# Stick-breaking attention by cumulated weights and differences of neighbouring values, in a decoder layer on one core

## The chip, the cores and the metric

The kernel runs on one core of a Trainium2 chip. The metric is the device time of one execution in microseconds (us). The kernel before was run three times: 3147.09 us in the median, 3140.37 lowest, 3151.94 highest.

Five engines work side by side, each through its own instruction stream in order: TensorE (PE in the profile, with PEld for its weight loads), VectorE (DVE), ScalarE (ACT), GpSimd (POOL) and SyncE (SP), which here issues nearly all DMAs.

## The reference, cut to what matters

One decoder layer on 2048 tokens of width 1024, in fp32: a normalised, modulated input is projected to queries, keys and values of 8 heads with forgetting attention ("fox") and 8 heads with stick-breaking attention ("sb"), each of width 64; both outputs are normalised per head and projected back, then follows a gated MLP with a short convolution, and a final norm. The change touches stick-breaking attention:

```python
z = einsum('bhqd,bhkd->bhqk', q_blk, k) * scale
strict = kpos[None, :] < qpos[:, None]
log_one_minus_beta = where(strict, log_sigmoid(-z), 0.0)
rest = cumsum(log_one_minus_beta, axis=3, reverse=True) - log_one_minus_beta
a = where(strict, exp(log_sigmoid(z) + rest), 0.0)
out = einsum('bhqk,bhkd->bhqd', a, v)
```

In words: with beta = sigmoid(z), key s gets the weight A(s) = beta(s) times the product of (1 - beta(j)) over all keys j between s and the query. Keys at or behind the query get none.

## The kernel before, in words

**Stages.** The attention stage comes first (0 to about 1600 us of the profile), then the output projection, the MLP's up-projection and its down-projection. The attention stage is a list of 32 units (L576), first 16 of sb, then 16 of fox: for each kind four head pairs p, and for each pair four blocks tb of 512 tokens. While a unit's attention (attend, L468) is recorded, the projection of the next unit (proj_gen, L580) is recorded between its steps by interleave (L131). A scheduler then orders the recorded instructions of each engine by a simulated timeline; each engine runs its list in that order. All matrix operands are split into a high part and a rest (split, L43: ACT writes the high part, then DVE or POOL subtracts).

**Projection of a unit** (finish_proj, L283). Queries and keys first (q, k), then, for even p, the values of two head pairs at once: matmuls at L320 into PSUM, then the split at L330 on ACT and DVE straight from PSUM into the tiles V (this pair) and V1, which L337 stores to DRAM for the next pair; for odd p, L307 loads it from there. For the first pair (sb, 0) the columns of the forget gate ride along, and each 128-token tile is done by itself (step 1); other even pairs do two tiles at a time. The input h comes through tiles named hp, 10 buffers; for (sb, 0) norm_proj (L353) computes them, and its split has its subtraction on POOL for tb > 0. Weights are split in load_w (L250), for sb with the subtraction on DVE (L252).

**Stick-breaking, one head and two query tiles of 128** (sb_head, L400). Keys go in chunks of up to 512 from the right (nearest to the query) to the left. For each chunk and query tile: two matmuls give -z in PSUM (L378, L379); ACT writes r = sigmoid(-z), which is 1 - beta, and a = sigmoid(z), which is beta (L410, L411). In the chunk on the diagonal (right is None) POOL sets one column to 0 (L415), and a DVE scan (L416) multiplies r up from the right, with a maximum against edge, whose identity part restarts it at the diagonal with 1. In a further chunk POOL copies the last product of the chunk to the right into the extra column (L418) and the scan (L419) goes on from it. Then a is multiplied by the product (L420): on DVE where (ch + qi) % 4 == 0, else on POOL. That is A.

**Weights times values** (weighted, L382), shared with fox: four 128x128 transposes on PE (L388) into PSUM, ACT copies the high part (L392), DVE subtracts (L393), and four matmuls (L397) with V add to the head's output. The head's end is L506 (ACT) and L507 (DVE), then head_var squares the output on POOL (L480).

**Queues.** SP issues the DMAs in its own order: q and k rearranged (L293, L303), hp (L346, L366), V (L307, L337), weights (L256). A DMA that has to wait holds those behind it on SP.

Of the kernel before, what the change touches and what calls it, by code (L numbers as in the profile page):

```python
# [8 lines left out]
F32 = mybir.dt.float32  # L9
# [3 lines left out]
ALU = mybir.AluOpType  # L13
# [3 lines left out]
P = 128  # L17
S = 2048
D = 1024
KT = D // P  # L20
HD = 64
NH = 8
NPAIR = 8
TB = 512
NTB = S // TB
# [8 lines left out]
def kernel(ctx: ExitStack, tc: tile.TileContext, x, c, w_ada, b_ada, g_attn, w_in, b_fgate,  # L34
                      g_out_fox, g_out_sb, w_out, g_mlp, w_up, conv_w, conv_b, w_down, g_final, out):
    nc = tc.nc
    x, out = x[0], out[0]
    w_ada, w_in, w_out, w_up, conv_w, w_down = w_ada[0], w_in[0], w_out[0], w_up[0], conv_w[0], w_down[0]

    def f(t):  # L40
        return t.bitcast(F32)

    def split(hi, lo, src, lo_engine=None):  # L43
        nc.scalar.activation(hi, src, AF.Copy)  # L44
        (lo_engine or nc.gpsimd).tensor_sub(lo, src, f(hi))  # L45

    const = ctx.enter_context(tc.tile_pool(name="const", bufs=1))
    dram = ctx.enter_context(tc.tile_pool(name="dram", bufs=1, space=DRAM))
# [7 lines left out]
    x1s = [dram.tile([P, D], F32, name=f"x1s{t}") for t in range(S // P)]  # L56
    vs = {k: [[dram.tile([P, 4, 2, P], F32, name=f"vs_{k}{p}_{t}") for t in range(NTB)] for p in range(2)]
          for k in ("sb", "fox")}
    zs = [dram.tile([4 * NH, P], F32, name=f"zs{t}") for t in range(NTB)]
    log_f = dram.tile([NTB * NH, TB], F32, name="log_f")  # L60
    fs = dram.tile([NH, S], F32, name="fs")
# [3 lines left out]
    edge = const.tile([P, TB + 1], F32, name="edge")  # L65
# [92 lines left out]
    sb = open_pool("sb", side="right")  # L158
    px = open_pool("px", side="right")
# [19 lines left out]
    def wide():  # L179
        return f(h_tile()).rearrange("p a n -> p (a n)")  # L180
# [68 lines left out]

    def load_w(kind, p):  # L250
        base = (0 if kind == "fox" else 3 * 512) + p * P
        lo_engine = nc.vector if kind == "sb" else None  # L252

        def load(tag, kt, first, step):
            raw = sl_.tile([P, 2, P], F32, name=f"raw_{tag}", tag="wraw", bufs=3)
            nc.sync.dma_start(raw, w_in[kt * P:(kt + 1) * P, first:first + (step + 1) * P].rearrange(  # L256
                "p (a n) -> p a n", n=P)[:, 0:step + 1:step, :])
            n = 2 * P + (NH if tag == "v" else 0)
            w_ = sl_.tile([P, 2, n], F32R, name=f"w_{tag}", bufs=8)
            w = w_[:, :, 0:2 * P].rearrange("p s (a n) -> p s a n", n=P)  # L260
            split(w[:, 0], w[:, 1], raw, lo_engine)
            if tag == "v" and (kind, p) == ("sb", 0):
                split(w_[:, 0, 2 * P:], w_[:, 1, 2 * P:], wfr[:, kt], nc.vector)
            return w if tag == "qk" else w_

        def load_qk(kt):
            qk_.append(load("qk", kt, base, 4))

        def load_v():
            return [load("v", kt, base + 1024, 1) for kt in range(KT)] if p % 2 == 0 else None  # L270

        qk_ = []
        if (kind, p) == ("sb", 0):
            return [qk_, load_qk, load_v]
        for kt in range(KT):
            load_qk(kt)
        return [qk_, load_v()]
# [5 lines left out]
    def finish_proj(kind, p, tb, aq, w, hts, res, ak=None):  # L283
        Q = sb.tile([P, 2, 2, TB], F32R, name="Q", bufs=2)
        K = sb.tile([P, 2, TB], F32R, name="K", bufs=5)
        V = sb.tile([P, 4, 2, P], F32R, name="V", bufs=6)
        q2 = sl_.tile([P, 2, TB], F32R, name="q2", bufs=2)
        k2 = sl_.tile([P, 2, TB], F32R, name="q2", bufs=2)
        nc.scalar.activation(q2[:, 0], aq, AF.Copy, scale=-HD ** -0.5)
        nc.vector.scalar_tensor_tensor(q2[:, 1], aq, -HD ** -0.5, f(q2[:, 0]), ALU.mult, ALU.subtract)  # L290
        for h in range(2):
            for r in range(2):
                nc.sync.dma_start(f(Q[r * HD:(r + 1) * HD, h]), f(q2[h * HD:(h + 1) * HD]))  # L293
        if ak is None:
            ak = pj()
            for kt in range(KT):
                accumulate(ak, 1, w[0], hts[kt], kt)
                if kt % 2:
                    yield
        split(k2[:, 0], k2[:, 1], ak, nc.vector)  # L300
        for h in range(2):
            for r in range(2):
                nc.sync.dma_start(f(K[r * HD:(r + 1) * HD, h]), f(k2[h * HD:(h + 1) * HD, r]))  # L303
        yield
        spill = vs[kind][p // 2][tb]
        if p % 2:
            nc.sync.dma_start(f(V), spill)  # L307
        else:
            V1 = sb.tile([P, 4, 2, P], F32R, name="V", bufs=6)
            forget = (kind, p) == ("sb", 0)  # L310
            step, width = (1, 2 * P + NH) if forget else (2, 2 * P)
            if forget:
                zn = px.tile([P, 4, NH], F32, name="zn", bufs=1)
            for i in range(0, 4, step):
                av = pj()
                for t in range(step):
                    tok = slice((i + t) * P, (i + t + 1) * P)
                    for kt in range(KT):
                        for m, (a, bb) in enumerate(((0, 0), (0, 1), (1, 0))):
                            nc.tensor.matmul(av[:, t * width:(t + 1) * width], hts[kt][:, a, tok],  # L320
                                             w[1][kt][:, bb, 0:width],
                                             start=kt == 0 and m == 0, stop=kt == KT - 1 and m == 2)
                        if kt % 4 == 3:
                            yield
                if forget:
                    nc.vector.tensor_copy(zn[:, i], av[:, 2 * P:width])
                av = av[:, 0:step * 2 * P].rearrange("p (t e h d) -> p t e h d", t=step, e=2, h=2)
                for e, v in enumerate((V, V1)):
                    v = v[:, i:i + step]
                    split(v[:, :, :, 0:HD], v[:, :, :, HD:P], av[:, :, e], nc.vector)  # L330
            if forget:
                b = pt()
                nc.tensor.transpose(b[0:4 * NH, 0:P], zn.rearrange("p t n -> p (t n)"), ident)
                zt = px.tile([4 * NH, P], F32, name="zt", bufs=1)
                nc.scalar.activation(zt, b[0:4 * NH, 0:P], AF.Identity, bias=bf_c)
                nc.sync.dma_start(zs[tb], zt)
            nc.sync.dma_start(spill, f(V1))  # L337
        res.append((Q, K, V))
        yield

    def proj(kind, p, tb, w, res):
        hts = []
# [57 lines left out]
    def sb_head(j, qc, hl, Q, K, V, o):  # L400
        n = (2 * j + 2 + 3) // 4
        right = [None, None]
        for ch in range(n - 1, -1, -1):
            at = []
            for qi in range(2):
                need = min(512, (2 * j + qi + 1) * P - ch * 512)
                b = logits(max(need, 2 * P), slice((qc + qi) * P, (qc + qi + 1) * P), hl, Q, K[ch])
                r = sx.tile([P, 512 + 1], F32, name="r", bufs=7)
                a = sx.tile([P, 512], F32, name="a", bufs=7)
                nc.scalar.activation(r[:, :need], b[:, :need], AF.Sigmoid)  # L410
                nc.scalar.activation(a[:, :need], b[:, :need], AF.Sigmoid, scale=-1.0)  # L411
                rev = r[:, 0:need + 1][:, ::-1]
                if right[qi] is None:

                    nc.gpsimd.memset(r[:, need:need + 1], 0.0)  # L415
                    nc.vector.tensor_tensor_scan(rev, rev, edge[:, TB - need:TB + 1][:, ::-1], 0.0, ALU.mult, ALU.max)  # L416
                else:
                    nc.gpsimd.tensor_copy(r[:, need:need + 1], right[qi][:, 0:1])  # L418
                    nc.vector.tensor_tensor_scan(rev, rev, rev, 1.0, ALU.mult, ALU.bypass)  # L419
                (nc.vector if (ch + qi) % 4 == 0 else nc.gpsimd).tensor_mul(a[:, :need], a[:, :need], r[:, 1:need + 1])  # L420
                right[qi] = r
                at.append(a)
            yield
            nk = min(4, 2 * j + 2 - 4 * ch)
            for m in range(0, nk, 2):
                kts = [4 * ch + m, 4 * ch + m + 1]
                weighted(o, kts, lambda kt, qi: at[qi][:, (kt - 4 * ch) * P:(kt - 4 * ch + 1) * P], V, hl,
                         ch == n - 1 and m == 0, ch == 0 and m == nk - 2, kts[0] == 2 * j)
                yield
# [225 lines left out]
    sx = open_pool("sx", side="right")  # L655
# [3 lines left out]
    for i, u in enumerate(units):  # L659
        kind, p, tb = u  # L660
# [3 lines left out]
        if u == ("fox", 0, 0):  # L664
            tick(1 << 20)
            close_pool("sx", "px")
            sx = open_pool("fx", side="right")
# [6 lines left out]
        if kind == "fox":  # L674
            n = sum(2 * (2 + 2 * tb + j2 + 1) for j2 in range(2)) + 1
        else:
            n = sum(2 * (tb + 1 + 2 * tb + j2 + 1) for j2 in range(2)) + 1
# [205 lines left out]
    for sblk in range(2):  # L883
# [21 lines left out]
        a, b = bank_a(), bank_a()  # L905
# [44 lines left out]
    for tb in range(NTB):  # L950
# [13 lines left out]
        for k in range(NKD):  # L964
            g, w = load(k, tb)
# [55 lines left out]
```

## Time and profile before

| | |
|---|---|
| time, median of 3 runs | 3147.09 us (3140.37 to 3151.94) |
| span of the profiled execution (no other time of it is listed) | 3139.3 us |
| PE busy | 2967.0 us, 95% |
| PE weight loads busy | 2511.6 us, 80% |
| DVE busy | 2145.5 us, 68% |
| ACT busy | 1691.0 us, 54% |
| POOL busy | 1227.1 us, 39% |
| mean granted TensorE clock | 0.983 |
| instructions | 46425 |

How to read it: busy time is the union of an engine's instructions. PE's matmuls overlap one another and their ends are modelled, so a busy PE isn't PE at its peak. Shares over the whole span mix stages: sb attention ends near 910 us, fox attention near 1600 us, and the rest is projections and MLP. A row of a group gives the line, the engine, the operation, output and inputs, the shape, the count, then busy us, mean ns of one, idle time of the engine ahead of it and what ended that. The line of a helper (split is L44 and L45) stands for all its callers; the tile names tell them apart.

### The profile page before, as it was taken

What the parts mean: (1) busy time and instruction counts of PE and PEld (TensorE: products, weight loads), DVE (VectorE), ACT (ScalarE), POOL (GpSimd) and SP (SyncE); (2) the same over time, 40 slices, a digit from 0 to 9 for tenths busy, and PEclk for the clock granted to TensorE, in tenths of its full rate; (3) what the DMA queues carried; (4) which work ended last, traced back from release to release, by engine and by line L of the source; (5) the groups of instructions that cost most, each with busy time, mean ns of one, the idle gap of its engine ahead of it and who ended that gap; (6) DMA issues with size and microseconds to landing.
All of it is one profiled execution on the core that took longest, in us unless ns stands there. A gap on an engine that the chain in (4) does not pass through costs nothing. (4 is left out here: it accounts for less than half of the span.)

```text
span 3139.3 us, 46425 instructions
## 1 busy us (share of the span) xinstructions
PE 2967.0 (95%) x15934; PEld 2511.6 (80%) x15934; DVE 2145.5 (68%) x3342; ACT 1691.0 (54%) x3161; POOL 1227.1 (39%) x1387
## 2 busy tenths in 40 slices
PE   6889998989989999999999999999899998999998
PEld 5778787877878889888877678888678887888887
DVE  6787888878875876556843587778987776354253
ACT  5666776666756676567744444444444444343332
POOL 1554455456553242242212344344444442322321
PEclk8999999999999999999999999999999999999999
DMA  9547542555336696585446632222222223554552
GB/s 267 177 140 255 168 136 69 182 185 155 123 108 221 214 314 211 158 313 162 164 158 222 212 97 86 86 83 83 82 82 89 85 81 130 190 199 161 189 199 90
DMA packets 292940, 496.51 MB, mean 158 GB/s; under 512 B 29448, under 2 KB 177664, under 8 KB 291680
## 3 DMA queue, kind: packets, MB, share of 16 engines
q1 hardware_dynamic: 281072, 480.92, 47.9%
q10 hardware_dynamic: 11632, 12.63, 1.1%
q8 instruction: 126, 2.06, 0.3%
q14 instruction: 110, 0.90, 0.1%
HBM read 352.61 MB, written 90.51 MB: 141 GB/s over the span
## 5 line engine op out<-in xcount | busy, mean ns | idle before, releaser
L810 PE MATMUL ps_o<-oa,wu 128*128 128x512 f32 x2088 | 503.5, 392 | 14.4 <-DVE oa L45 6.9
L810 PEld LDWEIGHTS ps_o<-oa,wu 128*128 128x128 f32 x2088 | 390.5, 188 | 105.5 <-DVE oa L45 10.7
L397 PE MATMUL ps_pv<-at,V 128*128 128x256 f32 x2304 | 410.9, 296 | 41.6 <-DVE at L393 24.8
L393 DVE TENSOR_TENSOR at<-ps_pt,at 128x512 fp32r<-128x512 f32 (+1 forms) x576 | 366.0, 653 | 102.8 <-ACT at L392 99.8
L281 PE MATMUL ps_pj<-hp,w_qk 128*128 128x512 f32 x1512 | 418.4, 406 | 11.1 <-ACT hp L44 3.1
L420 POOL TENSOR_TENSOR a<-a,r 128x512 f32<-128x512 f32 (+3 forms) x240 | 283.4, 1182 | 368.8 <-DVE r L416 112.3
L392 ACT ACTIVATE at<-ps_pt 128x512 fp32r<-128x512 f32 (+1 forms) x576 | 319.4, 577 | 179.8 <-PE ps_pt L388 147.3
L397 PEld LDWEIGHTS ps_pv<-at,V 128*128 128x128 f32 x2304 | 337.0, 192 | 84.6 <-DVE at L393 42.8
L281 PEld LDWEIGHTS ps_pj<-hp,w_qk 128*128 128x128 f32 x1512 | 275.7, 191 | 65.4 <-POOL hp L45 4.0
L45 DVE TENSOR_TENSOR wd<-wdraw,wd 128x1024 fp32r<-128x1024 f32 x88 | 112.4, 1277 | 261.4 <-ACT wd L44 261.4
L378 PE MATMUL ps_qk<-K,Q 128*128 128x512 f32 (+2 forms) x640 | 264.1, 414 | 11.3 <-DMA K<-q 5.8
L419 DVE TENSOR_TENSOR_SCAN r<-r 128x513 f32<-128x513 f32 x192 | 258.0, 1355 | 21.7 <-ACT r L410 14.5
L45 POOL TENSOR_TENSOR g<-graw,g 128x512 fp32r<-128x512 f32 x84 | 141.3, 1684 | 326.8 <-ACT g L44 326.8
L960 PE MATMUL ps_o<-wd,g 128*128 128x512 f32 x1040 | 250.8, 391 | 8.8 <-ACT g L44 8.8
L810 PE MATMUL ps_t<-ob,wu 128*128 128x512 f32 x984 | 243.2, 392 | 0.0
L320 PE MATMUL ps_pj<-w_v,hp 128*128 128x256 f32 (+1 forms) x1536 | 234.1, 291 | 4.8 <-DVE q L45 2.2
L379 PE MATMUL ps_qk<-K,Q 128*128 128x512 f32 (+2 forms) x640 | 238.1, 373 | 0.0
L960 PEld LDWEIGHTS ps_o<-wd,g 128*128 128x128 f32 x1040 | 196.2, 189 | 50.0 <-ACT g L44 9.2
L44 ACT ACTIVATE wu<-wuraw 128x512 fp32r<-128x512 f32 x214 | 133.2, 626 | 185.5 <-PE ps_o L810 111.5
L320 PEld LDWEIGHTS ps_pj<-w_v,hp 128*128 128x128 f32 x1536 | 211.8, 193 | 15.5 <-DVE q L45 3.1
L810 PEld LDWEIGHTS ps_t<-ob,wu 128*128 128x128 f32 x984 | 186.2, 189 | 39.4 <-DVE wu L45 0.3
L388 PE MATMUL ps_pt<-edge,a 128*128 128x128 f32 x1088 | 187.3, 281 | 27.6 <-POOL a L420 14.7
(217 smaller groups left out, 5743.3 us busy)
## 6 DMA issues: line engine op xcount, KB each, us to landing
hp<-hs SPq DMA_DIRECT2D x224, 512.0 KB
wuraw<-in_w_up_dram SPq DMA_DIRECT2D x84, 512.0 KB
wdraw<-in_w_down_dram SPq DMA_DIRECT2D x84, 512.0 KB
Q<-q SPq DMA_DIRECT2D x128, 256.0 KB
g<-u SPq DMA_DIRECT2D x42, 512.0 KB
graw<-g SPq DMA_DIRECT2D x84, 256.0 KB
hs<-hp SPq DMA_DIRECT2D x32, 512.0 KB
K<-q SPq DMA_DIRECT2D x128, 128.0 KB
```

The source lines that it names most:

```text
L45: (lo_engine or nc.gpsimd).tensor_sub(lo, src, f(hi))
L281: nc.tensor.matmul(acc, w[kt][:, a, n], h[:, bb], start=kt == 0 and i == 0, stop=kt == KT - 1 and i == 2)
L320: nc.tensor.matmul(av[:, t * width:(t + 1) * width], hts[kt][:, a, tok], w[1][kt][:, bb, 0:width], start=kt == 0 and m == 0, stop=kt == KT ...
L378: nc.tensor.matmul(b[:, :cw], Q[:, hl, 0, qcols], K[:, hl, :cw], start=True, stop=False)
L379: nc.tensor.matmul(b[:, :cw], Q[:, hl, 1, qcols], K[:, hl, :cw], start=False, stop=True)
L392: nc.scalar.activation(at[:, 0, lo:], b[:, lo:], AF.Copy)
L393: nc.vector.tensor_sub(at[:, 1, lo:], b[:, lo:], f(at[:, 0, lo:]))
L397: nc.tensor.matmul(o[:, 0:2 * P], V[kt // 4][:, kt % 4, hl, :], rhs, start=first and kk == 0 and w == 0, stop=last and kk == 1 and w == 1)
L419: nc.vector.tensor_tensor_scan(rev, rev, rev, 1.0, ALU.mult, ALU.bypass)
L420: (nc.vector if (ch + qi) % 4 == 0 else nc.gpsimd).tensor_mul(a[:, :need], a[:, :need], r[:, 1:need + 1])
L810: nc.tensor.matmul(b, w[:, p, j], o[:, q], start=first and i == 0, stop=last and i == 2, skip_group_check=True)
L960: nc.tensor.matmul(banks[t][n], g[:, a, t * P:(t + 1) * P], w[:, b, n * TB:(n + 1) * TB], start=k == 0 and i == 0, stop=k == NKD - 1 and i ...
```

## The change

With the cumulated weight C(s) = A(s) + A(s+1) + ... up to the query, summation by parts gives sum A(s) v(s) = sum C(s) (v(s) - v(s-1)), with v(-1) = 0. C follows the recurrence C(s) = beta(s) + (1 - beta(s)) C(s+1), from C = 0 at the query. So the scan becomes one multiply-add from the right, with r as the factor and a as the summand, written into a; the chunk to the right gives its first element as the scan's start value, by a pointer. Memset, column copy and product (L415, L418, L420) go. In the diagonal chunk POOL sets a to 0 where the key isn't ahead of the query (affine_select on the last 128 columns).

V now holds differences, split as before. For each sb value projection (p = 0 and 2, four blocks each) DVE copies the values from PSUM into an SBUF tile vr; SP stores vr to a DRAM buffer vd one row further down, stores its last row as the first of the next block's buffer, and loads the 512 rows from row 0 back as the tile before; POOL subtracts; then ACT and POOL split the difference into V and V1. The split's subtraction for the values moves from DVE to POOL, and that of the sb weights for p = 1, 2, 3 too.

```diff
+    vd = [[dram.tile([TB + 1, 2 * P], F32, name=f"vd{g}_{t}") for t in range(NTB)] for g in range(2)]
...
-        lo_engine = nc.vector if kind == "sb" else None
+        lo_engine = nc.vector if (kind, p) == ("sb", 0) else None
...
+            if kind == "sb":
+                vr = value_tile(p)
...
-                for e, v in enumerate((V, V1)):
-                    v = v[:, i:i + step]
-                    split(v[:, :, :, 0:HD], v[:, :, :, HD:P], av[:, :, e], nc.vector)
+                if kind == "sb":
+                    nc.vector.tensor_copy(vr[:, i:i + step], av.rearrange("p t e h d -> p t (e h d)"))
+                else:
+                    for e, v in enumerate((V, V1)):
+                        v = v[:, i:i + step]
+                        split(v[:, :, :, 0:HD], v[:, :, :, HD:P], av[:, :, e], nc.vector)
+            if kind == "sb":
+                steps_of_values(p // 2, tb, vr, V, V1)
+                yield
...
+    def value_tile(p):
+        t = wide() if p == 0 else px.tile([P, D], F32, name="xt", tag="xt", bufs=4)
+        return t.rearrange("p (i n) -> p i n", n=2 * P)
+
+    def steps_of_values(g, tb, vr, V, V1):
+        own = vd[g][tb]
+        nc.sync.dma_start(own[1:TB + 1].rearrange("(i p) n -> p i n", p=P), vr)
+        if tb == 0:
+            nc.sync.dma_start(own[0:1], edge[0:1, 0:2 * P])
+        if tb + 1 < NTB:
+            nc.sync.dma_start(vd[g][tb + 1][0:1], vr[P - 1:P, 3])
+        before = value_tile(2 * g)
+        nc.sync.dma_start(before, own[0:TB].rearrange("(i p) n -> p i n", p=P))
+        nc.gpsimd.tensor_sub(vr, vr, before)
+        dv = vr.rearrange("p t (e h d) -> p t e h d", e=2, h=2)
+        for e, v in enumerate((V, V1)):
+            split(v[:, :, :, 0:HD], v[:, :, :, HD:P], dv[:, :, e])
...
-                r = sx.tile([P, 512 + 1], F32, name="r", bufs=7)
+                r = sx.tile([P, 512], F32, name="r", bufs=7)
...
-                rev = r[:, 0:need + 1][:, ::-1]
                 if right[qi] is None:
-
-                    nc.gpsimd.memset(r[:, need:need + 1], 0.0)
-                    nc.vector.tensor_tensor_scan(rev, rev, edge[:, TB - need:TB + 1][:, ::-1], 0.0, ALU.mult, ALU.max)
-                else:
-                    nc.gpsimd.tensor_copy(r[:, need:need + 1], right[qi][:, 0:1])
-                    nc.vector.tensor_tensor_scan(rev, rev, rev, 1.0, ALU.mult, ALU.bypass)
-                (nc.vector if (ch + qi) % 4 == 0 else nc.gpsimd).tensor_mul(a[:, :need], a[:, :need], r[:, 1:need + 1])
-                right[qi] = r
+                    nc.gpsimd.affine_select(out=a[:, need - P:need], in_=a[:, need - P:need], pattern=[[-1, P]],
+                                            base=-1, channel_multiplier=1, compare_op=ALU.is_ge, fill=0.0)
+                rev = a[:, 0:need][:, ::-1]
+                nc.vector.tensor_tensor_scan(rev, r[:, 0:need][:, ::-1], rev,
+                                             0.0 if right[qi] is None else right[qi][:, 0:1], ALU.mult, ALU.add)
+                right[qi] = a
```

## The prediction

> **What bounds the kernel now.** I read first the page's busy shares in 40 slices of 78.5 us, to see the stages; the change touches only slices 1 to 12, the sb stage.
>
> ```profile
> PE   6889998989989999999999999999899998999998
> DVE  6787888878875876556843587778987776354253
> POOL 1554455456553242242212344344444442322321
> PEclk8999999999999999999999999999999999999999
> ```
>
> PE is at 8 or 9 tenths almost everywhere, DVE at 8 in the sb slices: two engines near their limit together. The sum by stretches says how near.
>
> ```profile
> core 0: us, PE busy (x) PEld busy (x) DVE busy (x) ACT busy (x) POOL busy (x), PEclk, DMA share, GB/s
> 130.00:910.00 780.00, 706.27 (x4485) 615.08 (x4484) 659.98 (x889) 528.71 (x1156) 419.42 (x595) 0.98 0.48 152
> 910.00:1580.00 670.00, 654.39 (x4300) 584.57 (x4298) 442.64 (x1137) 439.07 (x835) 211.97 (x283) 0.99 0.66 215
> ```
>
> The first row is sb, the second fox, the same kind of work on PE (logits, transposes, weighted values, projections). In sb PE is busy 90.5% and DVE 84.6%; in fox 97.7% and 66.1%. The change leaves PE's instructions as they are, so in this stage it can win at most PE's idle 73.7 us (780 - 706.3) and, to fox's share, 780 - 706.27/0.977 = 57 us. What ended the idle time is in the waits of PE from 100 to 910 us:
>
> ```profile
> PE ps_pv L397 <- DVE at L393: 23.3, 32, 1.3
> PE ps_pt L388 <- POOL a L420: 14.7, 20, 1.9
> PE ps_pv L397 <- DVE oT L507: 7.2, 7, 1.9
> ...
> PE ps_pt L388 <- DVE a L420: 2.3, 5, 0.6
> ```
>
> The columns are us in total, times, longest. The removed product is named for 17.0 us. The 30.5 us on L393 and L507 are waits for short DVE operations that stood behind longer ones in DVE's queue: they go with DVE's load, not with one line.
>
> **What DVE loses and gains.** Groups of DVE from 0 to 910 us (count, busy us, mean ns), then the single durations of the second scan (min, median, max):
>
> ```profile
> L419 DVE TENSOR_TENSOR_SCAN r<-r 128x513 f32<-128x513 f32 x192 | 258.0, 1355 | 21.7 <-ACT r L410 14.5 <-POOL r L418 4.1 <-POOL r L415 1.2
> L393 DVE TENSOR_TENSOR at<-ps_pt,at 128x512 fp32r<-128x512 f32 x222 | 146.5, 678 | 33.5 <-ACT at L392 32.7
> L420 DVE TENSOR_TENSOR a<-a,r 128x512 f32<-128x512 f32 x56 | 47.1, 841 | 4.2
> L416 DVE TENSOR_TENSOR_SCAN r<-r,edge 128x513 f32<-128x513 f32 x32 | 43.6, 1363 | 6.8 <-ACT r L410 6.6
> ...
> L45 DVE TENSOR_TENSOR w_qk<-raw_qk,w_qk 128x256 fp32r<-128x256 f32 x32 | 20.8, 660 | 5.4 <-ACT w_qk L44 5.2
> ...
> L45 DVE TENSOR_TENSOR V<-ps_pj,V 128x256 fp32r<-128x256 f32 x24 | 9.6, 408 | 0.9 <-ACT V L44 0.9
> L45 DVE TENSOR_TENSOR V<-ps_pj,V 128x128 fp32r<-128x128 f32 x32 | 8.9, 282 | 5.5 <-ACT V L44 5.3
> L45 DVE TENSOR_TENSOR w_v<-raw_v,w_v 128x256 fp32r<-128x256 f32 x16 | 7.9, 508 | 1.3 <-ACT w_v L44 1.3
> L420 DVE TENSOR_TENSOR a<-a,r 128x384 f32<-128x384 f32 x8 | 6.4, 804 | 0.5
> ...
> L420 DVE TENSOR_TENSOR a<-a,r 128x256 f32<-128x256 f32 x8 | 3.4, 423 | 0.5
> ...
> L420 DVE TENSOR_TENSOR a<-a,r 128x128 f32<-128x128 f32 x8 | 2.4, 306 | 0.4
> ```
> ```profile
> L419 DVE TENSOR_TENSOR_SCAN r<-r x192: 1192/1226/2309, 120.8 to 906.7; 128x513 f32<-128x513 f32 x192
> ```
>
> - The 80 products on DVE go: 47.1 + 6.4 + 3.4 + 2.4 = 59.3 us.
> - The scans stay, 320 of them, one element shorter. Multiply-add isn't in this trace; multiply-max with a second tensor (L416) and multiply alone (L419) cost the same, 1363 and 1355 ns, so the second operation costs nothing and I take 1226, the median of L419: its excess, 192 x 0.129 + 32 x 0.137 = 29 us, lies beside POOL's work, most of which goes, and I count 20. The bounds of this term: no excess lost (0), all lost (29); and a dearer addition (below).
> - Weight splits to POOL: 24 x 0.660 + 8 x 0.508 = 19.9 us.
> - The splits of the sb values go: 32 x 0.282 + 16 x 0.408 = 15.6 us. The copies from PSUM come: 16 of 128x256 at 0.408, the row of that shape, and 8 of 128x512 at 0.678, by L393, which reads PSUM in that shape; 12.0 us.
>
> Net 59.3 + 20 + 19.9 + 15.6 - 12.0 = 103 us off DVE, of 660. ACT's two splits of 512 columns in place of six or four smaller ones change it by some us either way, counted as nothing beside its 68% load in this stretch.
>
> **What POOL loses and gains.** The groups of POOL, 0 to 910 us, and the durations of the column copy:
>
> ```profile
> L420 POOL TENSOR_TENSOR a<-a,r 128x512 f32<-128x512 f32 x168 | 220.9, 1315 | 256.2 <-DVE r L419 84.7 <-ACT a L411 58.0 <-DVE r L416 24.2
> L418 POOL COPY r<-r 128x1 f32<-128x1 f32 x192 | 94.0, 492 | 1.9 <-DVE r L416 1.2
> L45 POOL TENSOR_TENSOR hp<-hf_a,hp 128x512 fp32r<-128x512 f32 x24 | 37.8, 1581 | 4.4 <-ACT hp L44 4.4
> ...
> masks.py:199 POOL TENSOR_SCALAR_AFFINE_SELECT edge<-edge 128x128 f32<-128x128 f32 x1 | 0.3, 294 | 0.1
> ```
> ```profile
> L418 POOL COPY r<-r x192: 176/186/2230, 118.0 to 905.6; 128x1 f32<-128x1 f32 x192
> ```
>
> 315 us go with the first two rows alone. In come 128 selects of 128x128 at 0.294 (38 us), 32 weight splits (20 us on DVE, here perhaps 25) and, for each of 8 value blocks, a subtraction of 1024 columns (2 x 1.32) and two of 512 (1.32 to 1.58), 5.5 us each, 44 in all. POOL falls from 419 to about 210 of 780 us; it is no bound. But L418's one column takes 186 ns in the median and 2230 at worst: a POOL instruction waits out a scan. The selects can be held likewise; each stands ahead of its scan, where a memset without a producer stood. Between 0.294 and 2.23 I take L418's mean excess of 0.3, or 0.6 us a select, and no net charge, as the product behind the scan, 1.3 us in the longest form, goes from the same chain. [...]
>
> **The values' new way through DRAM.** Before, one ACT and one DVE operation stood between a value matmul and V, the latter 0.28 or 0.41 us by the rows above. Now a copy, a store, a load, a subtraction and the splits follow. The nearest rows are in the order of time on SP, ACT and DVE:
>
> ```profile
> 284.11 0.32 SPq L239 DMA_DIRECT2D log_f<-fe  x1
> 284.52 1.80 SPq L346 DMA_DIRECT2D hp<-hs  x4
> 287.39 0.63 SPq L244 DMA_DIRECT2D fl<-log_f  x2
> ```
> ```profile
> 296.28 1.19 DVE L245 TENSOR_TENSOR_SCAN fc<-fl 8x512 f32<-8x512 f32 x1
> ```
> ```profile
> 1603.71 0.81 SPq L733 DMA_DIRECT2D x<-x1s  x2
> ...
> 1606.95 1.06 ACT L93 ACTIVATE junk_m<-x 128x1024 bf16<-128x1024 f32 x1 [2.09 <-DMA x<-x1s]
> ```
>
> A store that a load waits for takes at most 287.39 - 284.11 = 3.3 us; a 512 KB load 1606.95 - 1603.71 = 3.2 us; behind four loads of hp, a small one no more than 296.28 - 287.39 = 8.9 us. So the chain is 0.4 + 3.3 + 3.2 + 2.6 + 1.2 + 1.5 = 12 us, 18 with such traffic. The built program's order on PE has moved to meet it: in the first unit the first matmul on V stands behind 26 projection matmuls of 512 columns that stood behind it before, and some 40 transposes where there were some 20. By the next fences one such matmul is 226 ns (442 in 100 us of a saturated stretch) and a transpose 187.3/1088 = 0.17 us, so 26 x 0.226 + 40 x 0.17 = 13 us of PE work lie between the last value matmul and the first use, in place of some 3; the other even units are alike.
>
> ```profile
> 2300.00:2400.00 100.00, 100.00 (x442) 82.40 (x441) 78.25 (x88) 43.61 (x62) 46.56 (x33) 1.00 0.26 80
> ```
> ```profile
> L388 PE MATMUL ps_pt<-edge,a 128*128 128x128 f32 x1088 | 187.3, 281 | 27.6 <-POOL a L420 14.7
> ```
>
> Per block the lateness is between 0 and 18 - 13 = 5 us; I take 1, as the trip without traffic fits: 8 x 1 = 8 us of PE stall, bounds 0 and 40. What waits behind it: the subtraction waits for the load on POOL, and in the built order selects of the next chunks and the splits of hp stand behind it; a DVE scan waits for each select and PE for hp. On SP the load waits for the store, with loads or stores of hp behind it; hp has 10 buffers, of which two now hold vr and before in the first pair, so this is part of the same lateness.
>
> **The sum.** DVE's share in the stretch: (660 - 103)/748 = 74.5% (748 is the result, inserted). That is (84.6 - 74.5)/(84.6 - 66.1) = 0.55 of the way from sb's to fox's load; PE's share goes the same way from 90.5 to 94.4%, and 706.27/0.944 = 748: 32 us won. Of the 17.0 us of waits named for the product I add half, 8, since the scan becomes the last to come; less 8 for the values. 3139.3 - 32 - 8 + 8 = 3107 us of span. The median stands 3147.09 - 3139.3 = 7.8 us above the profiled span, for what lies around it and scatter, so the forecast is 3107 + 8 = **3115 us**.
>
> **The rivals.**
> - *More:* PE in sb comes to fox's share, 57 us, and the values' trip is covered: 3147 - 57 = 3090. For it, every engine but PE is relieved; against it, ACT stays at 68% in sb.
> - *Nothing to measure:* PE's idle time only changes its reason. Transposes, ACT's copy and L393 still follow each other, and L393's 23.3 us have ACT ahead of them as well as DVE. Half the win (16) less 16 at the values: 3147.
> - *Slower by the values' trip:* eight times POOL stands on the load with selects and hp behind it. At 7 us late each, 56, less the 40 won, 3147 + 16 = 3163. It decides above 5 us late (8 x 5 = 40), just the loaded chain's 18 us against the 13 of cover.
> - *The scan isn't what it was:* if the addition costs another step per element, half again on 1226 ns, 0.6 x 224 long scans plus short ones is some 150 us more on DVE, which would then be at 660 - 103 + 150 = 707 and the bound, where 660 filled 780: 780 x 707/660 = 836, 56 us more, 3203. [...] I give it little.
>
> **How the numbers follow.** Forecast (3099 to 3131) 0.48, more than that 0.20, nothing to measure 0.15, slower by the trip 0.14, by the scan 0.03. A measurement of this kernel tells about 0.5%, 16 us, from no change; so faster 0.68, same 0.15, slower 0.17. The range takes in the stronger win with the covered trip, a little below 3090, and the loaded trip: 3080 to 3165.
>
> **What would show it.** Right: PE's share from 130 us to the end of sb near 94%, that end some 30 us earlier, the scans at about 1.23 us, DVE near 75%, no L420; the stages behind unchanged. Wrong: waits of PE or of DVE's scans for POOL with the subtraction waiting on its DMA ahead of it; scans above 1.4 us; or PE's share unchanged with L393 still named.

## The result and the profile after

The changed kernel took **3105.34 us** in the median of four runs (3102.1 to 3111.93), beside 3146.06 us for the kernel before: a ratio of 0.9869, 95% interval 0.9852 to 0.9887. That is 41 us less, where 32 were forecast. The profiled execution has a span of 3103.7 us; its run took 2.2 us more.

The busy shares in 40 slices (now 77.6 us each), from the page of the changed kernel:

```profile
PE   6889999999999999999998899999899998999998
DVE  6787777787857765567733687778977776254253
POOL 1541321213131332341122344444444442332321
PEclk8999999999999999999999999999999999999999
```

In slices 4 to 11 PE is now at 9, DVE is mostly at 7 where it was mostly at 8, and POOL falls to 1 to 3. Where the time went is told by the first instructions of the stages: the first select of fox (first and last start are the two figures behind the durations) and the first matmuls of the down-projection, in the kernel before and in the changed one.

```profile
L446 POOL TENSOR_SCALAR_AFFINE_SELECT Fd<-Fb x128: 290/452/622, 930.1 to 1567.9; 128x128 f32<-128x128 f32 x32, 128x256 f32<-128x256 f32 x32, 128x384 f32<-128x384 f32 x32, 128x512 f32<-128x512 f32 x32
...
L960 PE MATMUL ps_o<-wd,g x1040: 389/389/796, 2657.3 to 3120.9; 128*128 128x512 f32 x174
```
```profile
L470 POOL TENSOR_SCALAR_AFFINE_SELECT Fd<-Fb x128: 294/458/624, 885.0 to 1527.1; 128x128 f32<-128x128 f32 x32, 128x256 f32<-128x256 f32 x32, 128x384 f32<-128x384 f32 x32, 128x512 f32<-128x512 f32 x32
...
L984 PE MATMUL ps_o<-wd,g x1040: 389/389/793, 2621.9 to 3085.3; 128*128 128x512 f32 x174
```

Fox begins 45.1 us earlier, the down-projection 35.4 us, and the span ends 35.6 us earlier: the whole win is in the sb stage. Behind it some 10 us were lost again in this trace, and 12 in the second trace of the changed kernel (fox 42.3 us earlier, the down-projection 30.0), against this one trace of the kernel before; the medians differ by 41. The sb stage up to the corresponding time, 910 - 45 = 865 us, by windows:

```profile
core 0: us, PE busy (x) PEld busy (x) DVE busy (x) ACT busy (x) POOL busy (x), PEclk, DMA share, GB/s
130.00:865.00 735.00, 692.86 (x4476) 604.63 (x4476) 580.97 (x764) 519.79 (x1134) 181.20 (x229) 0.99 0.54 169
```

PE stands at 94.3%, DVE at 79.0%, POOL at 24.7% (before: 90.5, 84.6, 53.8). The 45 us have two parts. PE's idle time fell from 73.7 us to 42.1, by 31.6. PE's busy time fell too, from 706.3 to 692.9, by 13.4, at nearly the same count of matmuls (4485 and 4476), with the granted clock (the share of TensorE's full clock that the profile says it was given) at 0.98 before and 0.99 now. By the trace's clock records it is 0.978 and 0.993, which on 706 us makes some 10, by an estimate. The second trace of the changed kernel says the same: 695.4 us busy and 42.6 idle from 130 to 868 us. The order of the matmuls changed as well, and no run separates it from the clock.

PE's waits from 100 to 880 us:

```profile
PE ps_pt L415 <- DVE a L443: 9.9, 22, 0.9
PE ps_pv L424 <- ACT at L419: 5.3, 2, 3.6
PE ps_qk L405 <- ACT a L438: 4.9, 7, 1.6
PE ps_pv L424 <- DVE at L420: 4.6, 12, 0.7
```

The wait for the short subtraction (L393, now L420) fell from 23.3 to 4.6 us. The wait for the product became one for the scan (L443), 9.9 in place of 17.0. The groups of DVE, then of POOL, 0 to 900 us:

```profile
L443 DVE TENSOR_TENSOR_SCAN a<-r,a 128x512 f32<-128x512 f32 x224 | 300.5, 1359 | 49.7 <-ACT a L438 30.7 <-POOL a L440 16.9
```
```profile
L440 POOL TENSOR_SCALAR_AFFINE_SELECT a<-a 128x128 f32<-128x128 f32 x128 | 52.0, 407 | 354.8 <-ACT a L438 338.5 <-PE ps_qk L406 6.5 <-DVE at L420 5.9
...
L45 POOL TENSOR_TENSOR V<-hp,V 128x512 fp32r<-128x512 f32 x8 | 12.5, 1580 | 0.0
L45 POOL TENSOR_TENSOR V<-xt,V 128x512 fp32r<-128x512 f32 x8 | 11.7, 1471 | 13.4 <-ACT V L44 12.9 <-DVE a L443 0.5
L363 POOL TENSOR_TENSOR hp<-hp 128x1024 f32<-128x1024 f32 x4 | 11.0, 2748 | 11.2 <-DMA hp<-vd 11.2
L363 POOL TENSOR_TENSOR xt<-xt 128x1024 f32<-128x1024 f32 x4 | 10.2, 2556 | 18.4 <-DMA xt<-vd 18.4
```

The long scans take 1359 ns in the mean, not 1226: as much as before. The subtractions and splits of the values on POOL have about the durations that were worked out; the selects take 407 ns in the mean where 294 was taken.

### The profile page after: what moved, and what is told of

Same layout as the page of the kernel before. It is cut to its first block, busy times and chain, and to the rows that moved or that the text cites. A ratio compares the mean times of both kernels' runs of the same rounds, so it can differ in the third digit from the quotient of the medians.

```text
span 3103.7 us, 45389 instructions
## 1 busy us (share of the span) xinstructions
PE 2955.7 (95%) x15934; PEld 2501.2 (81%) x15934; DVE 2071.3 (67%) x3206; ACT 1681.2 (54%) x3129; POOL 986.7 (32%) x1011
## 4 chain that ended last, share of the span: by engine, by line
PE 21%; DVE 10%; POOL 6%; DMA 6%; issue 5%; ACT 2%; SPq 0%; POOLq 0%; ACTq 0%; DVEq 0%
PE ps_o L984 8%; PE ps_t L984 4%; PE ps_bc L984 4%; DMA wuraw<-in_w_up_dram 3%; DVE wu L45 3%; PE ps_o L653 2%; PE ps_o L834 2%; DVE u L903 2%; POOL ws L822 2%; POOL wuraw L821 2%; POOL ws L820 1%; DVE u L924 1%; DVE u L902 1%; DMA r<-rstd 1%; PE ps_t L834 1%
## 5 line engine op out<-in xcount | busy, mean ns | idle before, releaser
L420 DVE TENSOR_TENSOR at<-ps_pt,at 128x512 fp32r<-128x512 f32 (+1 forms) x576 | 362.6, 650 | 96.5 <-ACT at L419 94.5
L443 DVE TENSOR_TENSOR_SCAN a<-r,a 128x512 f32<-128x512 f32 (+2 forms) x320 | 371.7, 1177 | 75.9 <-POOL a L440 41.1
L424 PE MATMUL ps_pv<-at,V 128*128 128x256 f32 x2304 | 397.9, 292 | 20.2 <-ACT at L419 9.4
L419 ACT ACTIVATE at<-ps_pt 128x512 fp32r<-128x512 f32 (+1 forms) x576 | 319.0, 578 | 132.8 <-PE ps_pt L415 106.3
L45 DVE TENSOR_TENSOR wd<-wdraw,wd 128x1024 fp32r<-128x1024 f32 x88 | 112.4, 1277 | 261.2 <-ACT wd L44 261.1
L437 ACT ACTIVATE r<-ps_qk 128x512 f32<-128x512 f32 (+2 forms) x320 | 173.6, 543 | 78.2 <-PE ps_qk L406 75.5
L44 ACT ACTIVATE wd<-wdraw 128x1024 fp32r<-128x1024 f32 x88 | 93.1, 1058 | 206.8 <-PE ps_bc L984 193.0
```

Of the source, the lines that this page charges most:

```text
L419: nc.scalar.activation(at[:, 0, lo:], b[:, lo:], AF.Copy)
L420: nc.vector.tensor_sub(at[:, 1, lo:], b[:, lo:], f(at[:, 0, lo:]))
L424: nc.tensor.matmul(o[:, 0:2 * P], V[kt // 4][:, kt % 4, hl, :], rhs, start=first and kk == 0 and w == 0, stop=last and kk == 1 and w == 1)
L443: nc.vector.tensor_tensor_scan(rev, r[:, 0:need][:, ::-1], rev, 0.0 if right[qi] is None else right[qi][:, 0:1], ALU.mult, ALU.add)
```

## The experiments

The theory to test was that of the forecast: DVE's lighter load wins about 32 us, the product's hop out of the chain 8, the values' trip costs 8. The rivals: the hop counts for most; POOL's load, which the forecast took for no bound, counts; the trip costs much more, or nothing.

**The changed kernel again.** No edit.

> The changed kernel once more, beside the next three on the same chip. All theories expect its 3105 us again, within 5 us.

3106.51 us (3100.96 to 3111.04), ratio 0.9875, interval 0.9859 to 0.989. The runs below are held against some 3106 us. One caution holds for all of them: the scheduler orders each edited kernel anew. Set side by side, the order of PE's matmuls up to 1000 us is the same in the two runs of the changed kernel (0.999 of it matches), but only 0.3 to 0.9 of it matches in the edited ones. So each difference below is the price of an edit with its new order, and no run holds the order fixed.

**No trip.**

```diff
-                if kind == "sb":
-                    nc.vector.tensor_copy(vr[:, i:i + step], av.rearrange("p t e h d -> p t (e h d)"))
-                else:
-                    for e, v in enumerate((V, V1)):
...
-            if kind == "sb":
-                steps_of_values(p // 2, tb, vr, V, V1)
-                yield
+                for e, v in enumerate((V, V1)):
+                    v = v[:, i:i + step]
+                    split(v[:, :, :, 0:HD], v[:, :, :, HD:P], av[:, :, e], nc.vector)
```

> The changed kernel without the values' way through DRAM: V holds the values themselves, split from PSUM by ACT and DVE as before, so the output is not the reference's (cumulated weights meet plain values). Theory of the prediction: the trip costs 8 us of PE stall in all, so this takes about 3097 us. Rival 1, the scheduler's new order covers the trip wholly: 3105 us within 4. Rival 2, the trip costs what its loaded chain said, up to 40 us: 3065 to 3085 us.

3087.26 us, ratio 0.9815, interval 0.9801 to 0.9828: **19 us** less than the changed kernel. So the new way of the values, with its copies, subtractions and splits, costs 19 us, not 8. None of the three expectations met it: it is not covered, and just short of the 3065 to 3085 us that the loaded chain said. PE's idle time in the sb stage fell to 28.2 us (of 717 from 130 us) and its busy time to 688.8, at a granted clock of 1.00.

**The products back, on the side and in the chain.** The first puts products of the removed shapes and counts back on the same engines (80 on VectorE, 240 on GpSimd), a times r into r, which nothing reads afterwards: it keeps the load and leaves the chain short. The second hands the product to the transposes.

```diff
+                (nc.vector if (ch + qi) % 4 == 0 else nc.gpsimd).tensor_mul(r[:, :need], a[:, :need], r[:, :need])
                 right[qi] = a
```

and in the second besides

```diff
-                at.append(a)
+                at.append(r)
```

> [...] Theory of load (the prediction's): VectorE's 59 us and the contention of GpSimd's 284 us made most of the win, so this loses 20 to 30 us: 3125 to 3135 us. Rival, theory of the chain: what counted is the product's hop between the scan and the transposes, so this stays within 6 us of 3105.

> As the run with products on the side, but the transposes read the product, so that it stands in the chain again as in the kernel before; the weights are then wrong by the factor r. Theory of load: 8 us more than the run with the product on the side, 3133 to 3143 us. Theory of the chain: 30 us or more above that run, near 3140 us. Both expect it near the kernel before, so it is the difference to the side run that tells.

On the side: 3181.59 us, ratio 1.0115 (1.0101 to 1.0129). In the chain: 3199.41 us, 1.0164 (1.015 to 1.0178). So the load alone costs 75 us and the hop in the chain another 18. The theory of the chain falls: load is four fifths. But both theories were far too small, and both runs end above the kernel before: what the change adds (19 us of trip and more) is in them without what it removes. The products on the side also hold the tiles r longer, but ScalarE waited for one of them for only 5.8 us in all. In the chained run PE's idle time in the sb stage is 96.5 us of 821, and its busy time 724.5 at a granted clock of 0.95: of the 86 us more than the changed kernel's 735, 32 are PE's own work taking longer.

**The two halves of the load.**

```diff
+                (nc.vector.tensor_mul(r[:, :need], a[:, :need], r[:, :need]) if (ch + qi) % 4 == 0 else None)
```

and, in the other run,

```diff
+                (nc.gpsimd.tensor_mul(r[:, :need], a[:, :need], r[:, :need]) if (ch + qi) % 4 else None)
```

> The changed kernel with only VectorE's 80 products put back on the side (a times r into r, read by nobody). With all 320 it took 3182 us, 75 above the changed kernel. Theory 1, VectorE's load sets it: 59 us of products cost about as much again, 3150 to 3170 us. [...]

> The changed kernel with only GpSimd's 240 products put back on the side. [...] Theory 2 (GpSimd's products): 3150 us or more, scans slower in the mean by 0.1 us or more, and waits of VectorE's scans for the select several times the 41 us that they were.

VectorE's 80 products: 3121.53 us, ratio 0.9919 (0.9905 to 0.9932), 15 us above the changed kernel and below the 3150 to 3170 us of the theory of VectorE's load. GpSimd's 240: 3151.23 us, 1.0016 (1.0005 to 1.0026), 45 above, in the 3150 or more of the theory of GpSimd's products. Both speak for that theory. The larger half is POOL's, an engine that even then has 482 of 770 us busy (100 to 870 us) and that PE hardly ever waits for by name. What lies between it and PE shows in the group of the long scans of that run (0 to 910 us) and in PE's wait for them (100 to 910 us; 9.9 us in the changed kernel):

```profile
L443 DVE TENSOR_TENSOR_SCAN a<-r,a 128x512 f32<-128x512 f32 x224 | 338.2, 1528 | 31.2 <-ACT a L438 18.2 <-POOL a L440 11.7
```
```profile
PE ps_pt L415 <- DVE a L443: 30.2, 49, 3.5
```

1528 ns in place of 1359: 224 x 0.169 = 38 us more on DVE from products that DVE neither runs nor waits for, and the shorter scans add 12. It is the overlap that does it: the 57 long scans during which POOL did nothing took 1.26 us in the mean, as the 153 of that kind in the changed kernel did (1.27); the 167 beside POOL's work took 1.62. The waits of DVE's scans for the select went from 41.1 to 56.0 us only, so the queue on POOL is the smaller part, against that expectation.

**The scan by its forms.** Four lines in place of one:

```diff
+                if right[qi] is None:
+                    nc.vector.tensor_tensor_scan(rev, r[:, 0:need][:, ::-1], rev, 0.0, ALU.mult, ALU.max)
+                elif ch % 2:
+                    nc.vector.tensor_tensor_scan(rev, r[:, 0:need][:, ::-1], rev, 0.0, ALU.mult, ALU.add)
+                elif qi:
+                    nc.vector.tensor_tensor_scan(rev, r[:, 0:need][:, ::-1], rev, right[qi][:, 0:1], ALU.mult, ALU.max)
+                else:
+                    nc.vector.tensor_tensor_scan(rev, r[:, 0:need][:, ::-1], rev, right[qi][:, 0:1], ALU.mult, ALU.add)
```

> The changed kernel with four forms of the scan on four lines: multiply-max from the constant 0 (diagonal chunks), multiply-add from the constant 0 (further chunks of odd number, which leaves out their carry), multiply-max and multiply-add from a pointer (chunks of even number). Long scans that meet no work of GpSimd took 1.22 us in the kernel before (513 elements, start value a constant) and 1.27 us in the changed one (512). If the pointer costs it: both pointer forms 1.27, both constant forms 1.21 to 1.22. If the addition costs it: both additions 1.27, both maxima 1.22. If only the two tensors in place of one do, or the trace's scatter: all alike.

One run: 3101.02 us. It leaves out part of the carries and takes maxima in place of sums, so only its durations are read here. The durations of the second and the fourth line (min, median, max), addition from a constant and from a pointer:

```profile
L446 DVE TENSOR_TENSOR_SCAN a<-r,a x64: 1187/1215/1571, 176.4 to 857.6; 128x512 f32<-128x512 f32 x64
```
```profile
L450 DVE TENSOR_TENSOR_SCAN a<-r,a x64: 1252/1277/2249, 121.3 to 859.3; 128x512 f32<-128x512 f32 x64
```

The multiply-max from a pointer lies at 1247/1282, with the other pointer form. So the addition costs nothing beside the maximum (1277 and 1282 ns), and the start value from a pointer costs 0.06 us a scan (1277 and 1215 ns): 192 x 0.06 = 12 us of DVE that the forecast didn't have. It also says why the scans look unchanged in the mean: most of what they gained from a quieter POOL the pointer took back. POOL's copy of the column (L418) is gone, but handing over the carry still costs, now on DVE.

**What in the trip costs.** First a shorter trip: one DMA from SBUF to SBUF, a partition further down.

```diff
-        nc.sync.dma_start(own[1:TB + 1].rearrange("(i p) n -> p i n", p=P), vr)
...
+        nc.sync.dma_start(before[1:P], vr[0:P - 1])
+        nc.sync.dma_start(before[0:1, 1:4], vr[P - 1:P, 0:3])
+        nc.sync.dma_start(before[0:1, 0], edge[0:1, 0:2 * P] if tb == 0 else vd[g][tb][0:1])
```

> The changed kernel with the values moved by one row straight from SBUF to SBUF in one DMA (plus three of one row), in place of a store to DRAM and a load behind it. The plain values without the trip saved 19 us. If the length of the trip is what costs (two DMAs in a row, the second waiting for the first), about half comes back: 3093 to 3099 us. If the POOL subtractions and splits behind it cost, or what stands behind them in GpSimd's queue, little comes back: 3102 to 3108 us.

3255.86 us, ratio 1.0346 (1.0331 to 1.0362): neither theory. POOL stood 19 us at the first block, and 20 to 25 at the seven others:

```profile
97.53 2.34 POOL L361 TENSOR_TENSOR hp<-hp 128x1024 f32<-128x1024 f32 x1 [19.04 <-DMA vd<-hp]
```

Then the same with the DMA cut in two, and that again with the pair that is needed first taken first:

```diff
-        nc.sync.dma_start(before[1:P], vr[0:P - 1])
+        nc.sync.dma_start(before[1:113], vr[0:112])
+        nc.sync.dma_start(before[113:P], vr[112:P - 1])
...
-        nc.gpsimd.tensor_sub(vr, vr, before)
...
+        for e, v in enumerate((V, V1)):
+            nc.gpsimd.tensor_sub(dv[:, :, e], dv[:, :, e], bv[:, :, e])
+            ...
+            split(v[:, :, :, 0:HD], v[:, :, :, HD:P], d, nc.vector if e == 0 else None)
```

> The run with the direct shift from SBUF to SBUF took 3256 us, since its DMA of 127 partitions held GpSimd some 20 us each time. Here it is cut in two, of 112 and of 15 partitions. [...] If SBUF to SBUF is slow in itself: above 3150 us.

> As the run with 112 and 15 partitions, and the differences of the pair that is needed first are taken and split first, with the rest on VectorE in place of GpSimd. If what follows the trip is part of the 19 us that the trip costs, another 3 to 6 us less than that run; if GpSimd's work there is covered, the same within 3 us.

Cut in two: 3113.0 us (3101.78 to 3119.08), ratio 0.9891 (0.9872 to 0.991). That is 143 us less than with one DMA of 127 partitions, and POOL stood 3.6 to 15.3 us ahead of the third pair's four subtractions, not 20 to 25: the theory that SBUF to SBUF is slow in itself, above 3150 us, falls. Why the one DMA of 127 stalled its reader, its partitions or something else in it, no run shows. But the trip, though shorter (by the order of time, 4.3 to 5.0 us from the end of the last copy to the subtraction in the first pair's blocks, where it was 7.0 to 8.9, and 9.0 to 15.2 in the third's, where it was 14.7 to 16.8), won nothing beside the changed kernel's 3106 us. With the needed pair first: 3107.21 us, 0.9877 (0.9862 to 0.9891). That is 6 us below the run before it, as the first theory said, but the intervals overlap, and it is no better than the changed kernel.

Last, a load that needn't wait for the store:

```diff
+        before = value_tile(2 * g)
+        nc.sync.dma_start(before, x[tb * TB:(tb + 1) * TB, 0:2 * P].rearrange("(i p) n -> p i n", p=P))
         nc.sync.dma_start(own[1:TB + 1].rearrange("(i p) n -> p i n", p=P), vr)
...
-        before = value_tile(2 * g)
-        nc.sync.dma_start(before, own[0:TB].rearrange("(i p) n -> p i n", p=P))
```

> The changed kernel, but the tile before is loaded from the input x (rows of no meaning here, so the output is not the reference's) instead of from the stored values: copies, stores, a load, subtractions and splits all stay, only the load no longer waits for the store. The run without the trip was 19 us faster than the changed kernel, and a shorter trip (112 and 15 partitions) brought nothing measurable. If the time from the values to their differences is what costs: 3086 to 3095 us. If the additional work and its place in the queues of VectorE, ScalarE and GpSimd cost, whatever the trip's length: 3102 to 3110 us.

3100.56 us (3096.02 to 3108.38), ratio 0.9868 (0.9848 to 0.9888): between the two theories, and by the intervals no difference from the changed kernel. It doesn't part them, for a reason not foreseen: the subtraction writes vr in place, so it still waits for the store that reads vr, 3.2 to 13.4 us behind the last copy.

**One sigmoid.**

```diff
-                nc.scalar.activation(a[:, :need], b[:, :need], AF.Sigmoid, scale=-1.0)
...
+                if right[qi] is None:
+                    nc.vector.tensor_tensor_scan(arev, rev, edge[:, TB - need:TB][:, ::-1], 0.0, ALU.mult, ALU.max)
+                else:
+                    nc.vector.tensor_tensor_scan(arev, rev, rev, right[qi][:, 0:1], ALU.mult, ALU.bypass)
```

> The changed kernel with a scan of the products themselves in place of the cumulated weights: one sigmoid, no select, the identity in the constant tile restarts the scan at the diagonal. The product from s to the query is 1 - C(s), so that the output lacks one term, the query's own value, and has the other sign; it is a bound of what ScalarE's 320 second sigmoids and the select ahead of the scan still cost. If TensorE is the bound by now: 3098 to 3106 us. If the chain from logits to scan counts (select 41 us, sigmoid 31 us of waits on VectorE): 3075 to 3095 us.

3091.72 us, ratio 0.982 (0.9806 to 0.9833), 15 us below the changed kernel, as the theory of the chain said: the select and ScalarE's second sigmoid still cost that much together. It leaves out the query's own value, whose addition would cost work on PE or DVE that wasn't tried. Of the kernels that compute the reference, none ran measurably faster than the changed one.

## Why the prediction was right, and where it was not

**Right in the outcome.** 3105 us lies in the range, the sign is right, and where 32 us against the median before were forecast, 41 came, all from the sb stage. Of the 10 us between the forecast and the result, 3 are the span (3107 forecast, 3103.7 measured) and 6 the term of 8 us between span and median: in the changed kernel the median lies 1.6 us above the profiled span. The profiled execution of the kernel before, 3139.3 us, lies below the lowest of its runs, 3140.37, so most of the 8 us was scatter.

**Right in the mechanism.** The route (less load on DVE, so shorter waits for its short operations, so a higher PE share) is what the traces show: L393's wait fell from 23.3 to 4.6 us, PE's share rose to 94.3% where 94.4 was worked out, and its idle time fell by 31.6 us. The scan's addition cost nothing (1277 ns from a pointer, 1282 with a maximum in its place), as the equal rows of L416 and L419 said; no run shows the dearer step per element, half again on the scan, that one rival assumed.

**What was luck.** The share of 94.4% was worked out from DVE at 74.5%. DVE came to 79.0%, and the prediction's own line from sb to fox gives 92.7% and 18 us of win for that. So the input of that step was wrong and its result right: PE gained more for DVE's load than the step gives, and the gain in idle time met the forecast by luck. The prediction also took PE's 706.27 us of work as fixed; it fell by 13.4 us with the higher granted clock or the new order, a term that the sum didn't have.

**The sizes of two terms were off, and their errors met.**
- *What the removed products are worth* was put at 32 + 8 = 40 us. Put back, they cost 93: 15 for VectorE's, 45 for GpSimd's, another 15 when both stand together, and 18 in the chain. The step that failed here is "POOL falls; it is no bound", with 20 us of contention at the scans: POOL's 240 products alone make the scans 38 us longer. These are prices in the changed kernel, whose scans have a select ahead of them, each with its own order; in the kernel before they may have been lower, and no run separates that. (POOL's load of about 210 us also left out 74 us of the rows that go, the shorter products and the memsets; it came to 181 even so, in part because the selects and the weights' splits took longer than counted.)
- *What the change adds* was put at 8 us. The run with the products in the chain differs from the kernel before by what the change adds, and by the memsets, column copies and splits that it takes off: 3199 - 3146 = 53 us, beside a busy POOL. Without the products it may be less. The trip is 19 of it, if it costs there what it costs in the changed kernel. The pointer's 12 us of DVE time and the select are further parts; how the other 34 us divide isn't settled. The run with one sigmoid puts the select and the second sigmoid together at 15.

**The trip was mis-sized, in part in its store.** The forecast took 3.3 us for a store that a load waits for, from a store of 64 KB, and 1 us of lateness for each block. In the first pair the store's issue to the load's takes 3.0 to 4.8 us, as forecast. The order of time on SP in the changed kernel, third pair:

```profile
530.06 0.38 SPq L356 DMA_DIRECT2D vd<-xt  x1
...
540.83 0.37 SPq L362 DMA_DIRECT2D xt<-vd  x1
```

10.8 us pass from the store's issue to the load's (10.2 to 10.9 in the four blocks), in the block shown with the store of a last row and loads of hp and of weights in between; from the last copy to the subtraction it is 7 to 9 us in the first pair's blocks and 15 to 17 in the third's, where the forecast's chain up to that point was 6.9, or 12.6 with traffic. That its length is what costs is not shown: the trips shortened by 2 to 4 us in the first pair and by 1 to 6 in the third (the run with 112 and 15 partitions) gave nothing beyond the scatter, and only the run without any trip, which also takes the copies, the subtractions and POOL's splits away, was faster.

**DVE's load.** 103 us less were worked out up to the end of sb; by the windows from 130 us it is 659.98 - 580.97 = 79. The missing 24 are mostly the scans: by their rows they fell from 375.3 to 372.6 us, 2.7 in place of 20, and the pointer's 12 us are most of that difference. Yet PE's idle time fell as forecast. That POOL's part, not in that sum, did the rest is likely by the run with GpSimd's products, but argued.

## What to carry to other kernels

An engine that nobody waits for can still cost time: POOL's 240 products lengthened DVE's long scans from 1359 to 1528 ns, and PE's wait for the scans rose from 9.9 to 30.2 us, so look at the spread of durations (1192 to 2309 ns for one shape) before calling a busy neighbour free. Price what a change adds by loaded rows of its kind too, not only by a small transfer in a quiet place. Don't take the main engine's busy time as fixed: here it moved by 13 us. And when a forecast lands, put the parts back one by one: here the removed products cost 93 us when put back, where 40 had been forecast, and a good sum hid it.

## What the runs showed of the hardware that was not expected

- A scan whose start value comes from a pointer takes 1277 ns where one from a constant takes 1215 (512 columns); add and max in the second operation cost the same (1277 and 1282 ns, both from a pointer).
- 240 two-input products on POOL make long scans on DVE 0.17 us slower in the mean (1359 to 1528 ns); scans without POOL's work beside them stay at 1.26 us.
- With a move from SBUF to SBUF in one DMA over 127 partitions of 4 KB its reader stood 19 to 25 us. With 112 and 15 partitions in two DMAs 4.3 to 5.0 us passed from the last copy to the subtraction in the first pair's blocks, and 9.0 to 15.2 in the third's.
- PE's matmuls of the sb stage took 724.5 us at a granted clock of 0.95 (products in the chain), 706.3 at 0.98 (before), 692.9 at 0.99 (changed) and 688.8 at 1.00 (no trip). PE idled 96.5, 73.7, 42.1 and 28.2 us there. Which causes which, no run here separates, and the clock isn't all of it: with one sigmoid it was 684.4 at 0.99.
